# PEER block of a two-block layer: expert columns in pieces of 256, routing search in pairs of heads, one comparison for both one-hots

## The chip, the core and the metric

The kernel runs on one core of one Trainium2 chip. The metric is device time in microseconds (us); lower is better. Three runs of the kernel before took 3589.3 to 3594.07 us, median 3592.75 us. The engines are named as in the profile: PE is TensorE, PEld its weight loads, DVE VectorE, ACT ScalarE, POOL GpSimd, SP SyncE (which here only issues DMAs).

## The reference, cut to what matters

Two blocks run on 256 tokens of 2048 features in float32. The change touches the PEER part of the second block alone: a product-key search picks 16 of 16384 experts for each of 8 heads and each token, and the experts' outputs are added with softmax gates.

```python
PEER_HEADS = 8; PEER_NKEYS = 128; PEER_HALF = 128; PEER_TOPK = 16
q = (xn @ w_pq).reshape(B, S, PEER_HEADS, 2, PEER_HALF)
s1 = jnp.einsum('bshd,hnd->bshn', q[..., 0, :], sub_k1)
s2 = jnp.einsum('bshd,hnd->bshn', q[..., 1, :], sub_k2)
v1, i1 = lax.top_k(s1, PEER_TOPK)
v2, i2 = lax.top_k(s2, PEER_TOPK)
cand = (v1[..., :, None] + v2[..., None, :]).reshape(B, S, PEER_HEADS, PEER_TOPK * PEER_TOPK)
vs, ci = lax.top_k(cand, PEER_TOPK)
e1 = jnp.take_along_axis(i1, ci // PEER_TOPK, axis=-1)
e2 = jnp.take_along_axis(i2, ci % PEER_TOPK, axis=-1)
eidx = e1 * PEER_NKEYS + e2
gates = jax.nn.softmax(vs, axis=-1)
# per token: act = gelu(expert_u[eidx] . x);  out = sum(act * gates * expert_v[eidx])
```

## The kernel before, in words

**Weights.** All large products run on PE with each operand split into a high and a low part. Weights stream from HBM in pieces of 512 KB. For each piece `_load` issues a DMA on the SP queue into `raw`, `_emit` lets ACT copy `raw` to `hi` and DVE subtract to get `lo`, and PE then uses both. `raw`, `hi` and `lo` have three buffers each, and `get` keeps two pieces ahead of the one that PE uses. While `self.share` is true, POOL makes the `lo` part of every second piece instead of DVE (line 341 in the trace).

**All experts are computed.** The kernel doesn't gather experts. It multiplies the tokens with all 16384 columns of `expert_u` (the u products: 32 quads of 512 experts, 8 pieces `w_u` each), applies Gelu, multiplies with a dense gate matrix that is zero where an expert isn't chosen, and multiplies the result with `expert_v` (the v products: 16 groups of 1024 experts, 16 pieces `w_v` each). `mmH` does the u products: per weight tile one matmul of 512 moving columns (line 390, `hi`) and one of 256 (line 391, `lo`). `mmB` does the v products with three matmuls (lines 362 to 364). A piece of `w_u` has 8 tiles of 128 rows and 128 columns; a piece of `w_pq` has 4 of 256 columns. Both need 16 matmuls.

**The gates.** `scores` finds the top 16 of each head's two key halves, as soon as a block of `w_pq` columns is done. `route` waits for all of these, then adds the candidates, finds their top 16 and picks the indices for four heads at a time, and makes `routeT` (the two indices and the gate of each of the 128 choices, per token). `dense` turns that into the gate matrix in 64 groups of 4 tokens: `onehot` builds `Bt` (one comparison on DVE, 512 columns) and `At` (four instructions on DVE that compare and multiply with the gate, 128 columns each), PE multiplies them (line 1977; four calls in the program, eight records in the trace), ACT copies the result from PSUM into `G`, and after every fourth group ACT issues a DMA that writes `G` to DRAM (`gdram`). When all 16 of these are written, `gated` can load a quad's gates `Gq` (on the SP queue), multiply them into the activations `act` on DVE, and split the result into `wh` (ACT) and `wl` (DVE), which a v group needs for its two quads.

**What sets the order.** The programs of the engines are written out by one Python thread. After each weight piece `pump` adds 2.6 to two credits, one for DVE and one for ACT, each held between -2 and 2, takes off what the meters of the two engines say was issued since (a fixed part, 0.066 for DVE and 0.2 for ACT, and a part per element), and runs steps of the waiting background tasks (`scores`, `route`, `dense`, `gated`) while both credits are positive. `finish(task)` runs a task to its end at once, and with it whatever it waits for; nothing else stands between. `peer_order` says which u quads and v groups follow each other: before, v group 0 comes after quad 11, then one v group after every second quad. Before a v group, `finish` is called for its two quads' `gated`. Every engine then executes its own program strictly in this order, and waits where a semaphore isn't there yet.

**Lines.** Every DVE and ACT instruction passes through the meter and so has line 37; they are told apart by their tiles.

Of the kernel before, what the change touches and what calls it, by code (L numbers as in the profile page):

```python
# [6 lines left out]
F32 = mybir.dt.float32  # L7
# [130 lines left out]
def layout(inp):  # L138

    f = {k: np.asarray(v) for k, v in inp.items()}  # L140
    A = {}
# [55 lines left out]
    eu = f["expert_u_2"][0].reshape(128, 128, 2, 8, 128)  # L197
    A["w_u"] = eu.transpose(0, 2, 4, 3, 1).reshape(256, 128, 1024)
# [867 lines left out]
LAG = 10  # L1066


class Block1(Mixers):
# [14 lines left out]
    def order(self):  # L1084
# [40 lines left out]
        for kind, i in self.peer_order():  # L1125
            if kind == "u":
                p("w_u", 8 * i, 8, kk=8, w=128)
            else:
                p("w_v", 16 * i, 16)
# [694 lines left out]
NACT = 11  # L1824
# [3 lines left out]
class Block3(Block2):  # L1828
    def peer(self, X):
        nc, V, S, G, A, bg, tc = self.nc, self.V, self.S, self.G, self.A, self.bg, self.tc  # L1830
        h, st = self.h, self.st
# [11 lines left out]
        v12 = rp.tile([128, 2, 2, 8, 16], F32, name="v12")  # L1843
        i12 = rp.tile([128, 2, 2, 8, 16], U32, name="i12")
        qT = [None] * 4

# [14 lines left out]
        def scores(c):  # L1861

            for t in range(2):
# [10 lines left out]
                for j in (0, 2):  # L1874
                    top16([(s[:, j + z], 128, v12[:, t, z, 2 * c + j // 2], i12[:, t, z, 2 * c + j // 2]) for z in range(2)])
                    yield

        self.share = True
        tk = []

        def take(i, ps):
# [5 lines left out]
            if z:  # L1887
                tk.append(bg.add(scores(c)))
# [6 lines left out]
        def route():  # L1895
            yield lambda: all(t[3] for t in tk)
            for t in range(2):
                f12 = rp.tile([128, 2, 8, 16], F32, name="f12")
                V.tensor_copy(f12, i12[:, t])
                cd = rp.tile([128, 4, 16, 16], F32, name="cand")  # L1900
                eq = cd.rearrange("p a b c -> p (a b c)").rearrange("p (m k) -> p m k", k=16)
                vs = rp.tile([128, 8, 16], F32, name="vs")
                ci = rp.tile([128, 8, 16], U32, name="ci")
# [228 lines left out]
```

## Time and profile before

| | |
|---|---|
| median of three runs | 3592.75 us |
| profiled execution, its own time | 3589.29 us |
| its span in the trace | 3587.5 us |
| PE busy | 3508.7 us (98%) |
| DVE busy | 2450.7 us (68%) |
| ACT busy | 1702.7 us (47%) |
| POOL busy | 383.6 us (11%) |

Times in the trace count from the start of the span. The pieces of `w_pq` are loaded from 1836 us on, those of `w_u` from 1932 us; the first v group's pieces from 2313 us. Busy shares are shares of the span. A matmul's record is as long as the matmul is in the array, and records overlap, so what a matmul costs is read from start to start of two that follow each other. A granted clock (PEclk) of 1.00 is 2.4 GHz, 0.5 is 1.2 GHz; a stretch in between had some of both. An idle time in brackets names what ended it.

### The profile page before, as it was taken

What the parts mean: (1) busy time and instruction counts of PE and PEld (TensorE: products, weight loads), DVE (VectorE), ACT (ScalarE), POOL (GpSimd) and SP (SyncE); (2) the same over time, 40 slices, a digit from 0 to 9 for tenths busy, and PEclk for the clock granted to TensorE, in tenths of its full rate; (3) what the DMA queues carried; (4) which work ended last, traced back from release to release, by engine and by line L of the source; (5) the groups of instructions that cost most, each with busy time, mean ns of one, the idle gap of its engine ahead of it and who ended that gap; (6) DMA issues with size and microseconds to landing.
All of it is one profiled execution on the core that took longest, in us unless ns stands there. A gap on an engine that the chain in (4) does not pass through costs nothing.

```text
span 3587.5 us, 47390 instructions
## 1 busy us (share of the span) xinstructions
PE 3508.7 (98%) x18330; PEld 2981.0 (83%) x18330; DVE 2450.7 (68%) x3245; ACT 1702.7 (47%) x1974; POOL 383.6 (11%) x404
## 2 busy tenths in 40 slices
PE   8899999999999999999999889899999999999999
PEld 8788877888888888889788778788888888888887
DVE  7987575466775577667667999766655656556665
ACT  4345543445554455545454455544444444444454
POOL 6900000000000000021214333100000000000000
PEclk9999999999999999999999999999999999999999
DMA  6455554665566555565455446666666666667765
GB/s 224 135 157 164 171 174 131 194 205 188 188 200 196 188 186 188 192 194 178 130 173 175 144 162 214 203 201 202 202 200 200 205 201 203 201 201 214 217 192 183
DMA packets 244794, 670.05 MB, mean 187 GB/s; under 512 B 86180, under 2 KB 86628, under 8 KB 242392
## 3 DMA queue, kind: packets, MB, share of 16 engines
q1 hardware_dynamic: 239144, 639.59, 56.2%
q10 hardware_dynamic: 2736, 17.32, 1.2%
q0 software_dynamic: 2688, 10.12, 1.0%
q8 instruction: 143, 2.34, 0.3%
q14 instruction: 83, 0.68, 0.1%
HBM read 648.07 MB, written 18.87 MB: 186 GB/s over the span
## 4 chain that ended last, share of the span: by engine, by line
PE 87%; DVE 9%; issue 1%; ACT 1%; DMA 1%; POOL 0%; SPq 0%; DVEq 0%; ACTq 0%; POOLq 0%
PE mm L390 21%; PE mm L362 16%; PE mm L363 16%; PE mm L364 16%; PE mm L391 11%; DVE lo L37 3%; DVE At L37 1%; PE mm L377 1%; PE mm L376 1%; PE mm L378 1%; PE m L1977 1%; DVE Bt L37 1%; ACT hi L37 1%; DVE cand L37 1%; PE m L492 1%
## 5 line engine op out<-in xcount | busy, mean ns | idle before, releaser
L37 DVE TENSOR_TENSOR lo<-raw,hi 128x1024 fp32r<-128x1024 f32 (+3 forms) x1123 | 1379.9, 1231 | 929.1 <-ACT hi L37 926.1
L37 ACT ACTIVATE hi<-raw 128x1024 fp32r<-128x1024 f32 (+1 forms) x1185 | 1247.0, 1054 | 1463.4 <-PE mm L364 806.7
L390 PE MATMUL mm<-xt,hi 128*128 128x512 f32 x3712 | 1319.9, 400 | 9.5 <-ACT hi L37 9.5
L391 PE MATMUL mm<-xt,lo 128*128 128x256 f32 x3712 | 1043.7, 281 | 15.2 <-DVE lo L37 14.9
L390 PEld LDWEIGHTS mm<-xt,hi 128*128 128x128 f32 x3712 | 701.5, 189 | 176.7 <-ACT hi L37 9.8
L391 PEld LDWEIGHTS mm<-xt,lo 128*128 128x128 f32 x3712 | 704.7, 190 | 19.3 <-DVE lo L37 18.3
L363 PE MATMUL mm<-lo,wh 128*128 128x512 f32 x1024 | 398.7, 389 | 1.3 <-DVE lo L37 1.3
L362 PE MATMUL mm<-hi,wh 128*128 128x512 f32 x1024 | 399.0, 390 | 0.6 <-ACT hi L37 0.6
L364 PE MATMUL mm<-hi,wl 128*128 128x512 f32 x1024 | 398.6, 389 | 0.0
L363 PE MATMUL mm<-lo,x 128*128 128x512 f32 x576 | 227.0, 394 | 10.1 <-DVE lo L37 10.1
L362 PE MATMUL mm<-hi,x 128*128 128x512 f32 x576 | 230.1, 399 | 2.7 <-ACT hi L37 2.7
L363 PEld LDWEIGHTS mm<-lo,wh 128*128 128x128 f32 x1024 | 192.2, 188 | 41.7 <-DVE lo L37 2.0
L364 PE MATMUL mm<-hi,x 128*128 128x512 f32 x576 | 226.1, 393 | 0.0
L362 PEld LDWEIGHTS mm<-hi,wh 128*128 128x128 f32 x1024 | 192.2, 188 | 40.7 <-ACT hi L37 1.0
L364 PEld LDWEIGHTS mm<-hi,wl 128*128 128x128 f32 x1024 | 192.2, 188 | 40.3
L341 POOL TENSOR_TENSOR lo<-raw,hi 128x1024 fp32r<-128x1024 f32 x62 | 159.5, 2572 | 336.9 <-ACT hi L37 296.6
L362 PE MATMUL mm<-hi,xt 128*128 128x512 f32 x376 | 147.2, 392 | 0.1
L363 PE MATMUL mm<-lo,xt 128*128 128x512 f32 x376 | 146.5, 390 | 0.0
L364 PE MATMUL mm<-hi,xt 128*128 128x512 f32 x376 | 146.4, 389 | 0.0
L363 PEld LDWEIGHTS mm<-lo,x 128*128 128x128 f32 x576 | 109.3, 190 | 34.1 <-DVE lo L37 12.6
L362 PE MATMUL mm<-hi,acth 128*128 128x512 f32 x352 | 137.2, 390 | 0.0
L364 PE MATMUL mm<-hi,actl 128*128 128x512 f32 x352 | 137.0, 389 | 0.0
(561 smaller groups left out, 4355.5 us busy)
## 6 DMA issues: line engine op xcount, KB each, us to landing
raw<-in_w_u_dram SPq DMA_DIRECT2D x256, 512.0 KB, 4.0
raw<-in_w_v_dram SPq DMA_DIRECT2D x256, 512.0 KB, 4.2
raw<-in_w_up_dram SPq DMA_DIRECT2D x176, 512.0 KB, 3.8
raw<-in_w_g_dram SPq DMA_DIRECT2D x96, 512.0 KB, 3.4
raw<-in_w_dn_dram SPq DMA_DIRECT2D x88, 512.0 KB, 4.3
raw<-in_w_o_dram SPq DMA_DIRECT2D x64, 512.0 KB, 3.4
raw<-in_w_b_dram SPq DMA_DIRECT2D x32, 512.0 KB, 3.6
raw<-in_w_br_dram SPq DMA_DIRECT2D x32, 512.0 KB, 3.4
```

What stands on the lines that cost most here:

```text
L37: return f(*a, **k)
L341: sub.tensor_sub(lo[:, ks], raw[:, ks], hi[:, ks].bitcast(F32))
L362: nc.tensor.matmul(ps[:, t, :n], xh[:, sl], hi[:, i, :n], start=s, stop=False)
L363: nc.tensor.matmul(ps[:, t, :n], xh[:, sl], lo[:, i, :n], start=False, stop=False)
L364: nc.tensor.matmul(ps[:, t, :n], xl[:, sl], hi[:, i, :n], start=False, stop=e)
L376: nc.tensor.matmul(ps[:, c, :], hi[:, i, sl], xh, start=s and c % 2 == 0, stop=False, **kw)
L377: nc.tensor.matmul(ps[:, c, :], hi[:, i, sl], xl, start=False, stop=False, **kw)
L378: nc.tensor.matmul(ps[:, c, :], lo[:, i, sl], xh, start=False, stop=e, **kw)
L390: nc.tensor.matmul(ps[:, c], hi[:, i, sl], xx, start=s, stop=False, **kw)
L391: nc.tensor.matmul(ps[:, c, 256:], lo[:, i, sl], xx[:, :256], start=False, stop=e, **kw)
L492: self.nc.tensor.transpose(ps[:, c, t * 128:t * 128 + 128], src(t)[:, c * 128:c * 128 + 128], self.ident)
L1977: nc.tensor.matmul(ps[:, i], Bs[:, i], As[:, i], start=True, stop=True)
```

## The change

What it does, in the order of the diff:

- `w_u` is laid out in pieces of 4 tiles of 256 columns instead of 8 of 128, and the u products use `prodH` as `w_pq` does.
- v group 0 comes after quad 14 (`FIRST` = 15) instead of after quad 11, and v group 1 follows it at once. The activations of the first four quads then lie in the pool `a4`.
- DVE's meter counts 0.15 as the fixed part from the PEER block on (0.066 before).
- A new background task `pairs` does the candidates' search for two heads and 128 tokens as soon as their scores are searched; `route` keeps the softmax and the transposes. Score tasks go ahead of the others.
- `onehot` makes both one-hots in one comparison of 1024 columns on DVE (tile `AB`); the multiplication with the gate becomes four copies of 128 columns on ACT, with a scale per partition.
- `share` ends before the first `w_u` piece is used instead of after `dense`. In the programs as built, POOL makes 16 `lo` parts instead of 62, all among the `w_pq` pieces.

```diff
-    eu = f["expert_u_2"][0].reshape(128, 128, 2, 8, 128)
-    A["w_u"] = eu.transpose(0, 2, 4, 3, 1).reshape(256, 128, 1024)
+    eu = f["expert_u_2"][0].reshape(64, 2, 128, 4, 4, 128)
+    A["w_u"] = eu.transpose(0, 3, 5, 4, 1, 2).reshape(256, 128, 1024)
...
-LAG = 10
+NACT = 11
+FIRST = NACT + 4
...
-                p("w_u", 8 * i, 8, kk=8, w=128)
+                p("w_u", 8 * i, 8, kk=4, w=256)
...
-        out, v = [], 0
-        for q in range(32):
+
+        out = [("u", q) for q in range(FIRST)] + [("v", 0), ("v", 1)]
+        v = 2
+        for q in range(FIRST, 32):
             out.append(("u", q))
-            if q >= LAG and (q - LAG) % 2 == 1:
+            if (q - FIRST) % 2 == 1:
                 out.append(("v", v))
                 v += 1
-        out += [("v", g) for g in range(v, 16)]
-        return out
+        return out + [("v", g) for g in range(v, 16)]
...
-NACT = 11
...
+        V.fixed = 0.15
...
         qT = [None] * 4
+        e3 = rp.tile([128, 2, 3, 8, 16], F32, name="e3")
+        v12 = rp.tile([128, 2, 8, 2, 16], F32, name="v12")
+        i12 = rp.tile([128, 2, 8, 2, 16], U32, name="i12")
...
-                for j in (0, 2):
-                    top16([(s[:, j + z], 128, v12[:, t, z, 2 * c + j // 2], i12[:, t, z, 2 * c + j // 2]) for z in range(2)])
+                for j in range(2):
+                    h = 2 * c + j
+                    top16([(s[:, 2 * j + z], 128, v12[:, t, h, z], i12[:, t, h, z]) for z in range(2)])
                     yield
+                tk.append(bg.add(pairs(c, t)))
+
+        def pairs(c, t):
+
+            hs = slice(2 * c, 2 * c + 2)
+            f12 = rp.tile([128, 2, 2, 16], F32, name="f12", bufs=2)
+            cd = rp.tile([128, 2, 16, 16], F32, name="cand", bufs=2)
+            eq = cd.rearrange("p a b c -> p (a b c)").rearrange("p (m k) -> p m k", k=16)
+            V.tensor_copy(f12, i12[:, t, hs])
+            V.tensor_tensor(cd, v12[:, t, hs, 0, :, None].to_broadcast([128, 2, 16, 16]),
+                            v12[:, t, hs, 1, None, :].to_broadcast([128, 2, 16, 16]), op=OP.add)
+            yield
+            ci = rp.tile([128, 2, 16], U32, name="ci", bufs=2)
+            top16([(cd[:, j].rearrange("p a b -> p (a b)"), 256, e3[:, t, 2, 2 * c + j], ci[:, j]) for j in range(2)])
+            yield
+            V.tensor_scalar(ab[:, 0], ci, 4, None, op0=OP.logical_shift_right)
+            V.tensor_scalar(ab[:, 1], ci, 15, None, op0=OP.bitwise_and)
+            V.tensor_copy(abf, ab)
...
+            for z in range(2):
+                V.tensor_tensor(eq, io16[:, None, :].to_broadcast([128, 32, 16]),
+                                abf[:, z].rearrange("p h j -> p (h j)")[:, :, None].to_broadcast([128, 32, 16]),
+                                op=OP.is_equal)
+                V.tensor_mul(cd, cd, f12[:, :, z, None, :].to_broadcast([128, 2, 16, 16]))
+                yield
+                V.tensor_reduce(e3[:, t, z, hs].rearrange("p h j -> p (h j)"), eq, axis=AX.X, op=OP.add)
+                yield
...
-                tk.append(bg.add(scores(c)))
+                bg.add(scores(c))
+                bg.tasks.insert(sum(x in bg.tasks for x in sc), bg.tasks[-1])
+                sc.append(bg.tasks.pop())
...
-            yield lambda: all(t[3] for t in tk)
+            yield lambda: all(t[3] for t in sc + tk)
+            mx = rp.tile([128, 2, 8, 1], F32, name="gmx")
+            V.tensor_copy(mx, e3[:, :, 2, :, 0:1])
             for t in range(2):
...
-                for g in range(2):
-                    hs = slice(4 * g, 4 * g + 4)
-                    V.tensor_tensor(cd, v12[:, t, 0, hs, :, None].to_broadcast([128, 4, 16, 16]),
-                                    v12[:, t, 1, hs, None, :].to_broadcast([128, 4, 16, 16]), op=OP.add)
-                    yield
-                    for h0 in (0, 2):
-                        top16([(cd[:, hh].rearrange("p a b -> p (a b)"), 256, vs[:, 4 * g + hh], ci[:, 4 * g + hh])
-                               for hh in (h0, h0 + 1)])
...
-                e3 = rp.tile([128, 3, 128], F32, name="e3")
...
-                        V.tensor_tensor(eq, io16[:, None, :].to_broadcast([128, 64, 16]),
-                                        abf[:, z, hs].rearrange("p h j -> p (h j)")[:, :, None].to_broadcast([128, 64, 16]),
-                                        op=OP.is_equal)
-                        yield
-                        V.tensor_mul(cd, cd, f12[:, z, hs, None, :].to_broadcast([128, 4, 16, 16]))
-                        yield
-                        V.tensor_reduce(e3[:, z, ms], eq, axis=AX.X, op=OP.add)
-                        yield
-                g3 = e3[:, 2].rearrange("p (h j) -> p h j", h=8)
+                g3 = e3[:, t, 2]
-                V.tensor_sub(g3, vs, vs[:, :, 0:1].to_broadcast([128, 8, 16]))
+                V.tensor_sub(g3, g3, mx[:, t].to_broadcast([128, 8, 16]))
...
-                    nc.tensor.transpose(ps[:, z], e3[:, z], self.ident)
+                    nc.tensor.transpose(ps[:, z], e3[:, t, z].rearrange("p h j -> p (h j)"), self.ident)
...
-                Bs = gp.tile([128, 4, 128], F32, name="Bt", tag="Bt", bufs=2)
-                As = gp.tile([128, 4, 128], F32, name="At", tag="At", bufs=2)
-                ts = slice(4 * n, 4 * n + 4)
-                V.tensor_tensor(Bs, self.iota[:, None, :].to_broadcast([128, 4, 128]),
-                                r_[:, 1, ts, None].to_broadcast([128, 4, 128]), op=OP.is_equal)
+
+                AB = gp.tile([128, 2, 4, 128], F32, name="AB", tag="AB", bufs=2)
+                V.tensor_tensor(AB, self.iota[:, None, None, :].to_broadcast([128, 2, 4, 128]),
+                                r_[:, 0:2, 4 * n:4 * n + 4, None].to_broadcast([128, 2, 4, 128]), op=OP.is_equal)
                 for i in range(4):
-                    t = 4 * n + i
-                    V.tensor_scalar(As[:, i], self.iota, r_[:, 0, t:t + 1], r_[:, 2, t:t + 1],
-                                    op0=OP.is_equal, op1=OP.mult)
-                return Bs, As
+                    S.activation(AB[:, 0, i], AB[:, 0, i], AF.Copy, scale=r_[:, 2, 4 * n + i:4 * n + i + 1])
+                return AB
...
+                AB = nxt
                 for i in range(4):
-                    nc.tensor.matmul(ps[:, i], Bs[:, i], As[:, i], start=True, stop=True)
...
-            self.room["W"] += 1
-            self.share = False
...
+        self.share = False
         for kind, i in self.peer_order():
             if kind == "u":
                 for z in range(2):
-                    ps = self.mm_ps([128, 2, 512])
-                    for e in range(2):
-                        for s in range(2):
-                            hi, lo = self.get("w_u")
-                            self.mmH(ps[:, e:e + 1], hi, lo, 8 * s, X, s == 0, s == 1)
-                            bg.pump()
+                    ps = self.prodH("w_u", X, 16)
                     if z == 0:
-                        if i >= NACT:
+                        if i >= FIRST:
                             bg.finish(wt[i - NACT])
-                        a = pact.tile([128, 4, 256], F32, name="act")
+                        a = self.a4([128, 4, 256], name="act") if i < FIRST - NACT else pact.tile([128, 4, 256], F32, name="act")
...
-            self.room["W"] += 2
+            self.room["W"] += 3 if i == 1 else 2
```

What becomes of the order, at three places. Names: `m_...` is the PSUM tile of a gate group; `mm` that of a product; numbers are the program's buffer numbers.

PE, in the last quad ahead of v group 0. Before (the last four of the last seven gate groups, in the middle of quad 11, then the next u piece):

```order
L1977 MATMUL m_19631<-At,Bt 128x128 x4
L1977 MATMUL m_19644<-At,Bt 128x128 x4
L1977 MATMUL m_19657<-At,Bt 128x128 x4
L1977 MATMUL m_19671<-At,Bt 128x128 x4
L390 MATMUL mm<-xt,hi 128x512
L391 MATMUL mm<-xt,lo 128x256
```

After (behind the last piece of quad 14 come 38 such gate rows, of which the last three stand here, and then v group 0):

```order
L1978 MATMUL m_20318<-AB 128x128 x4
L1978 MATMUL m_20330<-AB 128x128 x4
L1978 MATMUL m_20343<-AB 128x128 x4
L362 MATMUL mm<-hi,wh 128x512
L363 MATMUL mm<-lo,wh 128x512
L364 MATMUL mm<-hi,wl 128x512
```

Before, 7 gate groups stand together there, and the other 57 lie between u pieces; after, 38 stand together (rows `m_19876` to `m_20343`), and 26 lie between u pieces.

DVE, at the same place. Before:

```order
L37 TENSOR_TENSOR Bt<-iota,routeT 128x512
L37 TENSOR_SCALAR At<-iota,routeT 128x128 x4
L37 TENSOR_TENSOR Bt<-iota,routeT 128x512
L37 TENSOR_SCALAR At<-iota,routeT 128x128 x4
L37 TENSOR_TENSOR act<-act,Gq 128x1024
L37 TENSOR_TENSOR wl<-act,wh 128x1024
L37 TENSOR_TENSOR act<-mm,act 128x512
L37 TENSOR_TENSOR act<-act,R 128x512
L37 TENSOR_TENSOR lo<-raw,hi 128x1024 x4
L37 TENSOR_TENSOR act<-mm,act 128x512
```

After:

```order
L37 TENSOR_TENSOR lo<-raw,hi 128x1024 x2
L37 TENSOR_TENSOR AB<-iota,routeT 128x1024
L37 TENSOR_TENSOR lo<-raw,hi 128x1024
L37 TENSOR_TENSOR AB<-iota,routeT 128x1024
L37 TENSOR_TENSOR act<-mm,act 128x512
L37 TENSOR_TENSOR act<-act,R 128x512
L37 TENSOR_TENSOR AB<-iota,routeT 128x1024 x36
L37 TENSOR_TENSOR act<-act,Gq 128x1024
L37 TENSOR_TENSOR wl<-act,wh 128x1024
L37 TENSOR_TENSOR act<-act,Gq 128x1024
```

The `lo` parts, which before stand among the one-hots until shortly ahead of the end, are gone from the last 36 one-hots, and the four `At` instructions of a group have gone to ACT.

ACT, at the same place. Before:

```order
L37 ACTIVATE G<-m_19644 128x4x128
L1979 DMA gdram<-G 128x2048
L37 ACTIVATE G<-m_19657 128x4x128
L37 ACTIVATE G<-m_19671 128x4x128
L1990 DMA gdram<-G 128x2048
L37 ACTIVATE wh<-act 128x1024
L37 ACTIVATE act<-mm 128x512
L37 ACTIVATE hi<-raw 128x1024 x4
L37 ACTIVATE act<-mm 128x512
L37 ACTIVATE wh<-act 128x1024
```

After:

```order
L37 ACTIVATE AB<-AB,routeT 128x128 x4
L37 ACTIVATE G<-m_19842 128x4x128
L37 ACTIVATE hi<-raw 128x1024
L1980 DMA gdram<-G 128x2048
L37 ACTIVATE AB<-AB,routeT 128x128 x4
L37 ACTIVATE act<-mm 128x512
L37 ACTIVATE act<-act 128x1024
L37 ACTIVATE G<-m_19876 128x4x128
L37 ACTIVATE AB<-AB,routeT 128x128 x4
L37 ACTIVATE G<-m_19893 128x4x128
```

Four scaled copies (`AB<-AB,routeT`) now stand between two copies of `G`, and the last `hi` of the u pieces and of the first two v pieces stands ahead of all the 38 groups' copies of `G`.

## Rows read from the trace of the kernel before

**Rows 1.** Stretch, length, busy us (count) of PE, PEld, DVE, ACT, POOL; PEclk, DMA, GB/s.

```profile
1950.00:2100.00 150.00, 130.22 (x705) 110.59 (x703) 142.12 (x275) 62.51 (x67) 56.36 (x22) 0.97 0.46 151
2100.00:2305.00 205.00, 195.59 (x1266) 175.75 (x1267) 197.50 (x370) 120.78 (x127) 61.21 (x24) 0.99 0.55 195
2320.00:2340.00 20.00, 17.58 (x69) 13.90 (x70) 12.73 (x13) 8.02 (x10) 0.00 (x0) 0.82 0.67 188
...
2340.00:3410.00 1070.00, 1069.68 (x5285) 903.27 (x5284) 651.90 (x583) 478.91 (x478) 0.56 (x1) 1.00 0.67 204
```

**Rows 2.** What PE waited for, 1950 to 2340 us: us, times, longest.

```profile
PE mm L391 <- DVE lo L37: 14.9, 9, 3.3
PE mm L390 <- ACT hi L37: 9.5, 1, 9.5
```

**Rows 3.** PE's instructions by group, 1950 to 2320 us: count, busy us, mean ns.

```profile
L390 PE MATMUL mm<-xt,hi 128*128 128x512 f32 x738 | 271.1, 408 | 0.0
L1977 PE MATMUL m<-At,Bt 128*128 128x128 f32 x512 | 69.7, 279 | 7.7 <-DVE At L37 7.4 <-ACT G L37 0.3
```

**Rows 4.** PE in order of time (start, length): `w_pq`; then a gate group and `w_u`.

```profile
1882.36 0.39 PE L390 MATMUL mm<-xt,hi 128*128 128x512 f32 x1
...
1884.44 0.39 PE L390 MATMUL mm<-xt,hi 128*128 128x512 f32 x1
...
2295.13 1.95 PE L1977 MATMUL m<-At,Bt 128*128 128x128 f32 x16
...
2305.54 0.39 PE L390 MATMUL mm<-xt,hi 128*128 128x512 f32 x1
...
2310.05 0.40 PE L390 MATMUL mm<-xt,hi 128*128 128x512 f32 x1
```

**Rows 5.** DVE's instructions by group, 1833 to 2310 us.

```profile
L37 DVE TENSOR_SCALAR At<-iota,routeT 128x128 f32<-128x128 f32 x256 | 96.8, 437 | 0.0
L37 DVE TENSOR_TENSOR lo<-raw,hi 128x1024 fp32r<-128x1024 f32 x67 | 87.3, 1303 | 37.8 <-ACT hi L37 37.7
L37 DVE TENSOR_TENSOR Bt<-iota,routeT 128x512 f32<-128x512 f32 x64 | 56.8, 887 | 0.3 <-PE m L1977 0.3
```

**Rows 6.** ACT in order of time: scaled copies of 256 columns; a `G` and what follows.

```profile
16.99 0.89 ACT L37 ACTIVATE x<-xraw,mixg 128x256 fp32r<-128x256 f32 x2
...
2291.10 1.06 ACT L37 ACTIVATE G<-m 128x512 f32<-128x512 f32 x1 [2.63 <-PE m L1977]
2291.94 1.08 ACT L37 ACTIVATE hi<-raw 128x1024 fp32r<-128x1024 f32 x1
```

**Rows 7.** ACT by group, 1950 to 2345 us: an instruction of 128 columns without scale.

```profile
L37 ACT ACTIVATE e<-e 128x128 f32<-128x128 f32 x2 | 0.6, 310 | 7.9 <-DVE e L37 7.9
```

**Rows 8.** DVE in order of time, among the last gate groups.

```profile
2301.13 0.68 DVE L37 TENSOR_TENSOR Bt<-iota,routeT 128x512 f32<-128x512 f32 x1
2301.73 1.10 DVE L37 TENSOR_SCALAR At<-iota,routeT 128x128 f32<-128x128 f32 x4
2302.76 0.68 DVE L37 TENSOR_TENSOR Bt<-iota,routeT 128x512 f32<-128x512 f32 x1
```

**Rows 9.** The way from the last gate group to the first `wh` (engine q: its queue).

```profile
2303.84 1.17 PE L1977 MATMUL m<-At,Bt 128*128 128x128 f32 x8 [0.46 <-DVE At L37]
...
2306.13 0.33 ACTq L1990 DMA_DIRECT2D gdram<-G  x1
...
2310.14 0.39 SPq L2007 DMA_DIRECT2D Gq<-gdram  x1
...
2314.85 1.23 DVE L37 TENSOR_TENSOR act<-act,Gq 128x1024 f32<-128x1024 f32 x1 [10.39 <-DMA Gq<-gdram]
...
2316.11 1.06 ACT L37 ACTIVATE wh<-act 128x1024 fp32r<-128x1024 f32 x1 [10.01 <-DVE act L37]
```

**Rows 10.** PE in order of time, after its longest wait.

```profile
2322.08 0.63 PE L390 MATMUL mm<-xt,hi 128*128 128x512 f32 x1
...
2322.72 0.63 PE L390 MATMUL mm<-xt,hi 128*128 128x512 f32 x1
```

More of the change, by code (lines that the diff above doesn't have):

```diff
@@ L1873, in scores @@
                 yield
-                for j in (0, 2):
-                    top16([(s[:, j + z], 128, v12[:, t, z, 2 * c + j // 2], i12[:, t, z, 2 * c + j // 2]) for z in range(2)])
+                for j in range(2):
+                    h = 2 * c + j
+                    top16([(s[:, 2 * j + z], 128, v12[:, t, h, z], i12[:, t, h, z]) for z in range(2)])
                     yield
+                tk.append(bg.add(pairs(c, t)))
[11 more added lines that the diff above has]
+            yield
+            ab = rp.tile([128, 2, 2, 16], U32, name="ab", bufs=2)
+            abf = rp.tile([128, 2, 2, 16], F32, name="abf", bufs=2)
+            V.tensor_scalar(ab[:, 0], ci, 4, None, op0=OP.logical_shift_right)
[9 more added lines that the diff above has]
+                V.tensor_reduce(e3[:, t, z, hs].rearrange("p h j -> p (h j)"), eq, axis=AX.X, op=OP.add)
+                yield
         self.share = True
-        tk = []
+        sc, tk = [], []
         def take(i, ps):
@@ L1895, in route @@
         def route():
-            yield lambda: all(t[3] for t in tk)
+            yield lambda: all(t[3] for t in sc + tk)
+            mx = rp.tile([128, 2, 8, 1], F32, name="gmx")
+            V.tensor_copy(mx, e3[:, :, 2, :, 0:1])
             for t in range(2):
[L1898 to L1903, printed above, removed]
-                for g in range(2):
-                    hs = slice(4 * g, 4 * g + 4)
-                    V.tensor_tensor(cd, v12[:, t, 0, hs, :, None].to_broadcast([128, 4, 16, 16]),
-                                    v12[:, t, 1, hs, None, :].to_broadcast([128, 4, 16, 16]), op=OP.add)
-                    yield
-                    for h0 in (0, 2):
-                        top16([(cd[:, hh].rearrange("p a b -> p (a b)"), 256, vs[:, 4 * g + hh], ci[:, 4 * g + hh])
-                               for hh in (h0, h0 + 1)])
-                        yield
-                ab = rp.tile([128, 2, 8, 16], U32, name="ab")
-                abf = rp.tile([128, 2, 8, 16], F32, name="abf")
-                V.tensor_scalar(ab[:, 0], ci, 4, None, op0=OP.logical_shift_right)
-                V.tensor_scalar(ab[:, 1], ci, 15, None, op0=OP.bitwise_and)
-                V.tensor_copy(abf, ab)
-                yield
-                e3 = rp.tile([128, 3, 128], F32, name="e3")
-                for z in range(2):
-                    for g in range(2):
-                        ms, hs = slice(64 * g, 64 * g + 64), slice(4 * g, 4 * g + 4)
-                        V.tensor_tensor(eq, io16[:, None, :].to_broadcast([128, 64, 16]),
-                                        abf[:, z, hs].rearrange("p h j -> p (h j)")[:, :, None].to_broadcast([128, 64, 16]),
-                                        op=OP.is_equal)
-                        yield
-                        V.tensor_mul(cd, cd, f12[:, z, hs, None, :].to_broadcast([128, 4, 16, 16]))
-                        yield
-                        V.tensor_reduce(e3[:, z, ms], eq, axis=AX.X, op=OP.add)
-                        yield
-                g3 = e3[:, 2].rearrange("p (h j) -> p h j", h=8)
@@ L1974, in dense @@
                 ps = self.m1([128, 4, 128])
-                Bs, As = nxt
+                AB = nxt
                 for i in range(4):
-                    nc.tensor.matmul(ps[:, i], Bs[:, i], As[:, i], start=True, stop=True)
+                    nc.tensor.matmul(ps[:, i], AB[:, 1, i], AB[:, 0, i], start=True, stop=True)
                 if full is not None and n % 4 == 2:
```

2 lines of the change are left out of this document (removed).

## The prediction, made before the changed kernel was run

> **What bounds the kernel now.** I read the busy times by stretch first. From 2340 us to 3410 us PE is busy 1069.68 of 1070 us [rows 1]: there the kernel is its matmuls, and nothing that DVE, ACT or a DMA does faster shortens it. The time to win lies in the routing and the gates. Between 1950 and 2305 us DVE is busy 339.6 of 355 us and PE 325.8; from 2320 to 2340 us PE works at a granted clock of 0.82 on average [rows 1]. PE's own waits come next: it waits for `lo` parts that DVE is late with (14.9 us in 9 waits) and once for 9.5 us for a `hi` [rows 2], which stands in ACT's queue behind the first `wh`.
>
> How much PE loses in all is counted from its work. A pair of u matmuls (lines 390 and 391) takes 0.347 us from start to start (13 pairs from 2305.54 to 2310.05), a record of a gate matmul 1.95 / 16, less the last one's overhang, 0.111 us [rows 4]. From 1950 to 2320 us there are 738 pairs and 512 gate records [rows 3]: with 0.35 for a pair, since the first one after a gate group takes a little longer, 738 x 0.35 + 512 x 0.111 = 258 + 57 = 315 us, and 14 further small matmuls make 317. The stretch is 370 us long, so 53 us are lost. From 2320 to 2340 us, 2.4 us are idle and 18% of 20 us, 3.6 us, go to the half clock [rows 1], where a pair takes 0.64 us (2322.08 to 2322.72) [rows 10]. **Lost before: 59 us.** PE's total work is the same after (the number of matmuls doesn't change), so the new time is the old one, less 59, plus what PE loses then.
>
> **The change part by part.**
>
> *Pieces of 256.* 16 matmuls per piece either way. `w_pq` has the new form already: 6 pairs from 1882.36 to 1884.44 are 0.347 us each, as those of `w_u` are [rows 4]. DMA bytes and the ACT and DVE instructions per piece are the same too. I count 0; 0.001 us a pair would be 2 us over 2048 pairs, either way.
>
> *POOL's `lo` parts and the one-hots.* DVE gives up `At` (96.8 us) and `Bt` (56.8 us) [rows 5], takes 64 comparisons of 1024 columns at about 1.2 us (the `lo` of 1024 columns is the nearest form, 1.30 us on average with POOL beside it, [rows 5]) and 46 more `lo` parts at the same: -154 + 77 + 55 = -22 us. The search is only cut differently (two heads instead of four), and part of it moves into the `w_pq` pieces, where PE loses nothing that the rows show. With a larger fixed part in the meter, the order puts less DVE work after each piece. So the losses to a late `lo` between 1950 and 2300 us should nearly go; I leave 2 us (0 to 5), and 2 us for 26 changes between u and gate matmuls.
>
> *A new chain in the interleaved groups.* In a piece that carries a gate group ACT does `hi` (1.06), DVE `lo` (1.2) and the comparison (1.2), and ACT the four scaled copies, which stand ahead of the next `hi`: with 1.3 us for these, 4.8 us against 2.8 + 0.9 = 3.7 us of PE. In the order 26 groups fall on 37 pieces: 26 x 4.8 + 11 x 1.06 = 136 us against 37 x 2.8 + 26 x 0.9 = 127 us. Two pieces of lead (5.6 us) take up part of the 9. I take 4 us, between 0 and 12.
>
> *The burst.* This decides. After, the order has 38 of the 64 gate groups in one row between the last u piece of quad 14 and v group 0; before, 7. They are drawn there because `finish` asks for quad 0's `wh`, which needs all 16 blocks of `gdram`, and the credits allow only 26 groups by then, since a group now costs ACT 4 x 0.31 + 0.63 = 1.87 by its meter, and each piece's 2.6 has to pay 1.06 for a `hi` first. Between these groups PE has nothing else. Who sets their pace? On ACT four scaled copies and one `G`. The nearest scaled copy from SBUF to SBUF has 256 columns: two in 0.89 us, of which one lasts 0.49, so 0.40 from start to start [rows 6]. From 128 columns (0.31 us, [rows 7]) to the 1024 of `hi` (about 1.06) a column costs 0.00084 us, so 128 fewer take off 0.11: 0.29 us each. `G` lets the next instruction start 0.84 us after it [rows 6]. 4 x 0.29 + 0.84 + a quarter of a DMA issue of 0.33 [rows 9] = 2.08, say 2.1 us. DVE needs 1.2 us for a group and PE 8 x 0.111 = 0.89, both of which fit in. So 38 x 2.1 = 80 us, of which PE works 34: **46 us lost.** From below: copies as cheap as the unscaled one of 0.31 us with 0.1 overlap, 1.77 us a group, 33 us lost; from above: none overlaps, 2.7 us, 69 us. I take 46, nearest to the scaled row. At the head of the burst ACT first waits for the last u piece, adds, and does a Gelu: 2 us.
>
> Where the multiplication stands is also a rule of the Trainium skill (ScalarE: Activation LUTs, section Rules for kernel authors): multiplications belong on VectorE, not ScalarE. The rows of the burst before bear it out here: with compare and multiply in one DVE instruction a group takes 2302.76 - 2301.13 = 1.63 us [rows 8]. With that pace the 38 groups would lose 38 x (1.63 - 0.89) = 28 us and the sum below would be 18 us less; the order moves the multiplication to ACT, so 2.1 stands.
>
> *From the last group to the v products.* The way is the same as before, only nothing covers it: last gate matmuls from 2303.84 (0.9 us long), last `gdram` DMA at 2306.13 on ACT's queue, `Gq` from 2310.14 on SP's queue, DVE's multiplication at 2314.85, ACT's `wh` at 2316.11 to 2317.17 [rows 9]: 12.5 us. Before, two u pieces (5.6 us) ran in that time. Add 0.8 for `wl`, 3.5 for the half clock after such a pause (about 7 us of it were worked through before, at 0.64 instead of 0.35 a pair [rows 10]), and 1 for the third v piece, whose load now queues behind two `Gq` on SP. 18 us, between 14 and 24. On SP the first `Gq` moves behind 26 more weight loads; these are paced by `raw`'s three buffers and not by the queue, so that costs nothing, and POOL's queue has nothing left to delay. `Gq` of quads 2 and 3 come behind later loads with two pieces of lead: 0.
>
> **The sum.** Lost after: 2 + 2 + 4 + 46 + 2 + 18 = 74 us, against 59: +15 us. On the profiled execution's own 3589.3 us that gives 3604; the median of the runs lies 3.5 us above it, so I say 3607. What was won in the routing (about 40 us) is paid back in the burst.
>
> **Rivals.** (1) *The burst is cheap, faster than before.* If ACT's copies and `G` overlap so well that a group takes 1.4 us, the burst loses 19 us, the sum is 47 and the time 3577 to 3581. It turns to faster by over 0.2% at 38 x (p - 0.89) + 28 < 52, that is at p below 1.52 us. Against it: `G` alone takes 0.84 [rows 6], which leaves 0.15 for each copy beside the DMA issue, and no row of ACT has that. (2) *It evens out.* Copies at the unscaled price (1.77 us a group) and a way to the v products of 16 us: 2 + 2 + 4 + 33 + 2 + 16 = 59, which is no change, 3589 to 3593; with 1.95 us a group it is 7 us more. For it: both ends are in the rows. (3) *The chain also binds.* ACT to DVE and back with 4.8 us a piece in the interleaved part, where the lead is used up early, and ACT's waits for other engines break the overlap in the burst (2.3 us): 2 + 2 + 12 + 54 + 3 + 24 = 97, +38 us, 3627 to 3631. For it: every group needs two changes of engine more than before. (4) *The change doesn't do what it says*: gates ready at quad 15. By the order they aren't; that is the forecast itself.
>
> **How the numbers follow.** 0.2% of the time, about 7 us, is what a measurement of this kernel can tell from no change. Forecast (3600 to 3617) 0.53, chain and slow burst (up to 3636) 0.24, even (3586 to 3600) 0.16, faster 0.07. So slower 0.77, same 0.16, faster 0.07. The range leaves out the fast rival and part of the even case below and the end of the slow one above: 3592 to 3632.
>
> **What would show it.** In the trace after: line 391's waits for DVE's `lo` gone between 1950 and 2300 us (right: under 5 us); 304 records of the gate matmuls without a u matmul among them, 75 to 90 us long, ACT busy throughout and PE under half; groups 2.0 to 2.2 us apart; then a pause of 12 to 14 us that ends with `wh`. POOL with 16 `lo` parts. Wrong would be: groups under 1.6 us apart; PE waits for `hi` or `lo` of over 15 us among the first 26 groups; or PE waiting after 2450 us, where I expect none beyond the 0.3 us of before.

## The result and the profile after

The kernel after takes 3621.13 us (median of 4 runs, 3619.2 to 3624.63) against 3591.11 us: a ratio of 1.0084, 95% interval 1.0066 to 1.0101. It is slower, inside the range, by 30 us where 15 were forecast. The profiled execution took 3624.63 us, its span 3622.8 us, 35.3 more than the span before. The busy time by stretch (us of PE, PEld, DVE, ACT, POOL, then granted clock, DMA share, GB/s), to be read beside [rows 1]:

```profile
1950.00:2180.00 230.00, 227.49 (x1300) 197.72 (x1299) 195.17 (x400) 107.95 (x116) 0.00 (x0) 1.00 0.57 183
2180.00:2337.00 157.00, 143.31 (x841) 124.11 (x840) 89.91 (x85) 103.70 (x186) 0.00 (x0) 0.98 0.47 158
2345.00:2416.00 71.00, 49.16 (x282) 42.49 (x282) 43.75 (x36) 71.00 (x180) 0.00 (x0) 0.96 0.32 131
2416.00:2440.00 24.00, 11.54 (x40) 8.82 (x40) 7.58 (x7) 7.51 (x9) 0.00 (x0) 0.64 0.77 221
2440.00:3440.00 1000.00, 998.51 (x4883) 840.76 (x4882) 611.07 (x543) 443.76 (x441) 0.56 (x1) 1.00 0.66 205
```

In the routing PE now works nearly throughout. Among the interleaved gate groups (2180 to 2337 us) its records leave 14 us free (its starts, below, show 22 lost) though neither DVE nor ACT is full. In the row of groups ACT is busy for 71.00 of 71 us. Behind it come the pause and the half clock, and from 2440 us on PE is idle for 1.5 of 1000 us, next to nothing, as before. PE's waits between 1830 and 2500 us (total us, times, longest) and what ACT waits for, to be read beside [rows 2]:

```profile
ACT AB L37 <- DVE AB L37: 54.5, 27, 2.9
PE m L1978 <- ACT AB L37: 36.6, 46, 4.2
PE mm L362 <- ACT wh L37: 12.4, 1, 12.4
PE mm L391 <- DVE lo L37: 6.2, 9, 1.1
```

The wait for `lo` has shrunk from 14.9 to 6.2 us; in its place PE waits for ACT's scaled copies, and ACT for the comparison: 27 times, about once for each of the 26 groups that lie among u pieces.

One measure serves all kernels below: **PE's loss** in a stretch is the sum, over neighbouring matmuls, of the time from start to start less the usual time of the same two lines (0.233 + 0.117 us for a pair, 0.112 for a gate record). Usual is the lowest of the kernels' medians, so that a wait which one kernel always has at some place doesn't count as usual. "Routing" is 1830 us to the first gate matmul, "among" the gate groups between u pieces, "row" those without u matmuls between, with the wait at its head, "way" the 60 us after the last gate matmul. The kernel before has such a wait in its routing, at the small matmuls of the softmax (1950 to 2340 us):

```profile
PE m L1943 <- DVE e L37: 7.1, 2, 4.2
```

The expectations below leave it out: they reckon with 25.6 us for the routing before, and with 57 for the sum.

| kernel | routing | among | row (groups) | way | sum | median us |
|---|---|---|---|---|---|---|
| before | 32.0 | 12.7 | 3.4 (7) | 15.8 | 63.9 | 3591.1 |
| after | 7.9 | 22.2 | 47.2 (38) | 15.9 | 93.2 | 3621.1 |
| e1_behind | 8.4 | 3.1 | 43.6 (40) | 14.7 | 69.7 | 3597.9 |
| e3_oldhot | 5.4 | 1.3 | 32.9 (42) | 15.2 | 54.8 | 3583.3 |
| e7_newhot | 30.2 | 17.7 | 35.7 (33) | 15.3 | 98.9 | 3628.4 |
| e6_lag10 | 7.6 | 3.3 | 61.2 (57) | 15.1 | 87.2 | 3615.9 |
| e4_route | 45.6 | 13.9 | none | 16.5 | 76.1 | 3596.2 |
| e13_fixed | 11.4 | 8.4 | 23.2 (34) | 15.3 | 58.2 | 3587.2 |
| e5_share | 23.5 | 30.0 | 30.4 (24) | 14.3 | 98.2 | 3626.7 |
| e15_nopool | 5.3 | 1.8 | 27.6 (40) | 17.7 | 52.3 | 3576.1 |
| e8_pieces | 31.5 | 15.2 | 3.5 (7) | 15.6 | 65.8 | 3588.8 |
| e14_rate | 6.1 | 5.6 | none | 12.9 | 24.7 | 3550.8 |
| e17_high | 5.8 | 11.4 | none | 11.0 | 28.2 | 3555.4 |
| e18_oldsearch | 2.0 | 5.6 | none | 10.0 | 17.6 | 3543.7 |

The sums follow the spans of the profiled executions within some 6 us: after less before is 29.3 by the sums and 35.3 by the spans. Of the 6 us between them 3 lie ahead of all that was changed, since the first `w_pq` matmul starts at 1850.9 instead of 1847.8 us.

### The profile page after: what moved, and what is told of

It is laid out like the page before. It is cut to its first block, busy times and chain, and to the rows that moved or that the text cites. A ratio compares the mean times of both kernels' runs of the same rounds, so it can differ in the third digit from the quotient of the medians.

```text
span 3622.8 us, 47446 instructions
## 1 busy us (share of the span) xinstructions
PE 3523.5 (97%) x18330; PEld 2988.6 (82%) x18330; DVE 2407.5 (66%) x3088; ACT 1769.2 (49%) x2228; POOL 261.9 (7%) x358
## 4 chain that ended last, share of the span: by engine, by line
PE 88%; DVE 5%; ACT 4%; issue 2%; DMA 2%; POOL 0%; SPq 0%; ACTq 0%; DVEq 0%
PE mm L390 22%; PE mm L362 15%; PE mm L363 15%; PE mm L364 15%; PE mm L391 11%; ACT AB L37 2%; DVE lo L37 2%; PE mm L377 1%; PE mm L376 1%; PE mm L378 1%; ACT G L37 1%; ACT hi L37 1%; DVE AB L37 1%; PE m L858 1%; PE m L492 1%
## 5 line engine op out<-in xcount | busy, mean ns | idle before, releaser
L37 DVE TENSOR_TENSOR lo<-raw,hi 128x1024 fp32r<-128x1024 f32 (+1 forms) x1169 | 1431.3, 1227 | 963.1 <-ACT hi L37 959.9
L362 PE MATMUL mm<-hi,wh 128*128 128x512 f32 x1024 | 400.3, 391 | 12.4 <-ACT wh L37 12.4
L363 PE MATMUL mm<-lo,x 128*128 128x512 f32 x576 | 227.1, 394 | 14.1 <-DVE lo L37 13.9
L363 PE MATMUL mm<-lo,acth 128*128 128x512 f32 x352 | 137.0, 389 | 0.0
```

What stands on the lines that cost most here:

```text
L37: return f(*a, **k)
L362: nc.tensor.matmul(ps[:, t, :n], xh[:, sl], hi[:, i, :n], start=s, stop=False)
L363: nc.tensor.matmul(ps[:, t, :n], xh[:, sl], lo[:, i, :n], start=False, stop=False)
```

## The experiments

### Among the groups: a chain over two engines

The timeline of one group among u pieces in the kernel after (start, us, engine; in brackets the idle time before and its releaser):

```profile
2300.15 1.28 ACT L37 ACTIVATE AB<-AB,routeT 128x128 f32<-128x128 f32 x4 [2.49 <-DVE AB L37]
2300.61 1.36 PE L1978 MATMUL m<-AB 128*128 128x128 f32 x8 [0.24 <-ACT AB L37]
2301.34 1.04 ACT L37 ACTIVATE hi<-raw 128x1024 fp32r<-128x1024 f32 x1
2302.41 1.23 DVE L37 TENSOR_TENSOR lo<-raw,hi 128x1024 fp32r<-128x1024 f32 x1 [2.35 <-ACT hi L37]
2303.55 1.22 DVE L37 TENSOR_TENSOR AB<-iota,routeT 128x1024 f32<-128x1024 f32 x1
2304.86 1.28 ACT L37 ACTIVATE AB<-AB,routeT 128x128 f32<-128x128 f32 x4 [1.51 <-DVE AB L37]
2305.32 1.36 PE L1978 MATMUL m<-AB 128*128 128x128 f32 x8 [0.53 <-ACT AB L37]
```

The next copies start 4.71 us after these: copies, `hi`, `lo`, comparison, copies, with DVE idle for 2.35 us in between and ACT for 1.51. The chain was in the prediction (4.8 us); what it costs PE was not. If this reading is right, the copies need only go behind the next `hi`:

```diff
+                    yield 1
+                    scaled(n + 1, nxt)
```

(`scaled` holds the four copies that stood at the end of `onehot`.)

> The kernel after, with one thing moved: the four scaled copies of a gate group are issued on ACT one piece later than the comparison, so behind the next hi and no longer ahead of it. By the order 24 groups then lie between u pieces and 40 in one row (27 and 37 in the kernel after). Theory A (the 24.7 us lost among the interleaved groups are the chain: copies wait for the comparison, the comparison stands behind lo, lo waits for hi, hi stands behind the copies): the chain is cut, at most 5 us stay, and three more groups in the row cost 3 us: 3621 - 20 + 3 = about 3604 us, and ACT's waits for the comparison among the interleaved groups fall from 2 us each to nearly none. Theory B (they are lost because DVE now makes every lo part alone and is late with lo and comparison): nothing is gained, 3621 to 3625 us. On both the row of groups keeps its 1.96 us a group.

3597.88 us, 1.0023 times before (1.0014 to 1.0033); 22.2 us among the groups became 3.1, and ACT's waits for the comparison fell as foretold:

```profile
ACT AB L37 <- DVE AB L37: 6.9, 10, 2.9
```

Theory B falls: DVE had as many `lo` parts to make as before this edit. Then the one-hots of the kernel before in the kernel after (the diff's block `onehot` taken back):

> The kernel after with the one-hots of the kernel before: DVE makes one comparison for Bt and four compare-and-multiply instructions for At, ACT makes nothing of them. By the order 22 groups lie between u pieces and 42 in one row. Theory A (ACT's part in the one-hots is what costs, by its place in the chain and by the pace of 1.96 us): chain 24.7 -> 4 us, the 42 groups at the 1.63 us of the row before lose 42 x 0.74 = 31 us instead of 37, head of the row 9.5 -> 3: about 3621 - 33 = 3588 us. Theory B (DVE is the late engine among the interleaved groups, since POOL gives it no help): the old one-hots take DVE longer, so the interleaved groups lose 25 us or more, and the total is 3609 us or more.

3583.30 us, 0.998 (0.997 to 0.999), 38 us under the kernel after. A group in the row costs 0.78 us instead of 1.24 (each with its share of the head). And the other way round, the new one-hots alone in the kernel before:

> The kernel before with the new one-hots alone (one comparison of both on DVE, four scaled copies on ACT); search, meter, POOL, pieces and order as before. By the order 31 groups lie between u pieces and 33 in one row. Theory A (a group with its copies on ACT costs PE 0.8 us among u pieces by the chain and 1.1 in a row by ACT's pace): routing 25.6 as before, among 31 x 0.8 = 25 instead of 13, row 33 x 1.1 + 8 = 44 instead of 3, way 16: 111 against 57, about 3644 us. Theory D (DVE is the engine that runs late, and what it is relieved of helps): no more lost among u pieces than the 13 us of before, 3620 us or less.

3628.42 us, 1.0111 (1.0094 to 1.0128): 38 us slower. Theory D falls; theory A was too high by 16 us: 7 among the u pieces, where a group cost 0.57 us and not 0.8, and 8 in the row, 35.7 us and not 44. **The new one-hots alone cost about as much as they cost in the kernel after.**

### The order of u and v

`peer_order` and the first `W` room taken back to those of before:

> The kernel after with the order of u and v groups of the kernel before (first v group after quad 11). By the order 7 groups lie between u pieces and 57 in one row, and one more quad of u pieces follows the row ahead of the first v group. Theory A (a group costs PE about 1 us wherever it lies, 0.9 among u pieces by the chain and 1.0 in the row by ACT's pace, and only the way to the v products depends on the order): row 57 x 1.01 = 58, interleaved 7 x 0.9 = 6, routing 5, head 9, way 4 with the u quad as cover, sum 82 against 93 of the kernel after: about 3610 us. Theory C (the long row of groups comes from putting v later, and costs only there): the row gets longer by 20 groups but starts earlier, and the total is near the kernel before, 3591 us or less; or, if the row alone counts, 3621 + 20 = 3641 us.

3615.91 us, 1.0071 (1.0053 to 1.0089): 5 us under the kernel after. The row of 57 costs 1.07 us a group, so a group costs about the same wherever it lies, and theory C falls. Missed was the way: 15.1 us, not 4, though four u pieces lie behind the row. PE waits 9.6 us for their `hi`, which stands behind the first `wh` in ACT's queue, as in the kernel before [rows 2].

### The routing: which part brought the 24 us?

First the new search alone in the kernel before (`scores`, `pairs`, `take`, `route` of the diff):

> The kernel before with the new search alone: pairs of heads, the sums and indices of two heads begun as soon as their scores are there; one-hots, POOL, pieces and order stay as before. Theory A: of the 30 us that PE loses between 1830 and 2100 us in the kernel before, 5 stay, as in the kernel after: 3591 - 25 = 3566 us. Theory B (the search only gains in the kernel after because the meter's larger fixed part puts less DVE work after a piece): the DVE work moves into the w_pq pieces, lo parts are late there instead, and the gain is under 8 us: 3583 to 3591 us.

3596.21 us, 1.0018 (1.0009 to 1.0028): both theories fall, the kernel is 6 us slower. In its trace the routing loses 13.6 us more, 5.4 of them in PE's waits for `qT`, which the kernel before doesn't have; but that execution took 3604.61 us, 8 above the median. Then the meter's line alone:

```diff
+        V.fixed = 0.15
```

> The kernel before with one line of the change: the meter's fixed part for a DVE instruction raised from 0.066 to 0.15 us in this stage. Search, one-hots, POOL's lo parts, pieces and order stay. By the order the routing's DVE work is spread over more pieces, 30 gate groups lie between u pieces and 34 in one row (7 before). Theory M (the larger fixed part alone is what makes room for the lo parts in the routing): PE's loss from 1830 us to the first gate matmul falls from 25.6 us to 8, as in the kernel after; the row loses 34 x 0.78 = 27 us instead of 3, among the u pieces 8 instead of 13, the way to the v products 16 as before: 59 lost against 57, about 3592 us. Theory P (POOL's lo parts are what is late in the routing): the 25.6 us stay, and the row comes on top: about 3610 us.

3587.17 us, 0.9987 (0.9978 to 0.9997): the routing falls to 11.4 us, near what theory M has, and the row pays it back. But the kernel after with POOL's `lo` parts given back (`self.share = False` moved to the end of the gates) speaks against M as the whole of it:

> The kernel after with POOL making every second lo part until the gates are done, as in the kernel before. By the order 40 groups lie between u pieces and 24 in one row. Theory M (the meter made the room in the routing): the loss in the routing stays at 8 us; 40 groups among u pieces lose 0.82 us each by the chain, 33 us; the row 24 x 1.1 + 9 = 35; way to the v products 16: 92 us, about 3620 us. Theory P (POOL's lo parts come late): the routing loses 25 us again, and groups whose lo POOL makes lose more than 0.82 us each: 3637 us or more.

3626.65 us, 1.0107 (1.009 to 1.0124), between the two theories: with the same meter and search the routing loses 23.5 instead of 7.9 us. The trace shows longer instructions. The same DVE groups from 1955 to 2110 us (busy us, mean ns, then DVE's idle time before them), first of the kernel after, without POOL:

```profile
L37 DVE TENSOR_TENSOR act<-act,R 128x512 f32<-128x512 f32 x13 | 9.0, 692 | 0.4
L37 DVE TENSOR_TENSOR act<-mm,act 128x512 f32<-128x512 f32 x13 | 8.9, 687 | 3.7 <-ACT act L37 3.6
L37 DVE TENSOR_TENSOR cand<-io,abf 128x512 f32<-128x512 f32 x9 | 6.2, 688 | 0.1
L37 DVE CAST f<-i 128x64 f32<-128x64 uint32 x5 | 0.9, 189 | 0.0
```

then of e5_share, with POOL:

```profile
L37 DVE TENSOR_TENSOR act<-act,R 128x512 f32<-128x512 f32 x13 | 16.9, 1296 | 0.4
L37 DVE TENSOR_TENSOR act<-mm,act 128x512 f32<-128x512 f32 x13 | 8.9, 681 | 3.2 <-ACT act L37 3.2
L37 DVE TENSOR_TENSOR cand<-io,abf 128x512 f32<-128x512 f32 x13 | 14.2, 1091 | 0.2
L37 DVE CAST f<-i 128x64 f32<-128x64 uint32 x6 | 8.3, 1384 | 0.0
```

Instructions with two inputs, both from SBUF, last up to twice as long on average, a small cast seven times. The one that reads `mm` from PSUM does not change, nor does the sum over `cand`, with one input (679 and 680 ns). So one more run, POOL's `lo` parts taken from the kernel before from the first u piece on, and nothing else:

```diff
         ssp = self.ssp5 = self.small([128, 2, 4], "ssp")
+        self.share = False
```

> The kernel before with POOL making no lo parts from the first u piece on; search, meter, one-hots, pieces and order stay. By the order 40 gate groups then lie in one row. Theory Q (POOL's lo parts give DVE nothing: where POOL works, DVE's two-input instructions from SBUF last longer, lo 1.42 instead of 1.22 us, act x R 1.14 instead of 0.69, so what DVE must make itself it gets back in shorter instructions): the loss in the routing stays near the 25.6 us of before, within 6 us, the row of 40 loses 40 x 0.78 + 2 = 33, among the u pieces 5, way 15: 79 against 57, 3608 to 3616 us. Theory R (DVE loses the help and is later): routing 40 us or more, 3625 us or more. Theory P (POOL was what delayed the routing): routing 10 us or less, 3597 us or less.

3576.05 us, 0.9961 (0.9945 to 0.9976), with the old search and the old meter: the routing loses 5.3 us, and the kernel is 14 us faster though 40 groups now lie in a row. Theory P, on which I had not bet, is right in its numbers: **without POOL's help `lo` is hardly late.** From 1955 to 2110 us (columns as in the first view above), in the kernel before and then in e15_nopool:

```profile
1955.00:2110.00 155.00, 133.56 (x716) 113.50 (x715) 147.25 (x261) 61.98 (x67) 57.84 (x22) 0.96 0.46 150
```

```profile
1955.00:2110.00 155.00, 153.27 (x872) 132.77 (x871) 146.72 (x280) 74.36 (x80) 0.00 (x0) 1.00 0.56 184
```

DVE is busy equally long, 147 us, but PE gets through 872 matmuls instead of 716. In the kernel before, eight groups of DVE instructions last longer there than in e15_nopool, 31 us in sum. Two of them in the kernel before and then in e15_nopool:

```profile
L37 DVE TENSOR_TENSOR lo<-raw,hi 128x1024 fp32r<-128x1024 f32 x22 | 31.1, 1415 | 6.8 <-ACT hi L37 6.8
L37 DVE TENSOR_TENSOR act<-act,R 128x512 f32<-128x512 f32 x11 | 12.6, 1144 | 0.4
```

```profile
L37 DVE TENSOR_TENSOR lo<-raw,hi 128x1024 fp32r<-128x1024 f32 x54 | 64.9, 1218 | 5.4 <-ACT hi L37 4.2 <-PE m L1943 1.0
L37 DVE TENSOR_TENSOR act<-act,R 128x512 f32<-128x512 f32 x14 | 9.7, 693 | 0.5
```

The 31 us are more than the 22 x 1.22 = 27 us which POOL's 22 `lo` parts spare DVE: this much of theory Q holds. The meter counts what POOL spares and not what it costs, so the program puts more on DVE than fits.

The order changes as well: without POOL the meter charges every `lo` to DVE, and the routing spreads over 63 u pieces ahead of the first gate group instead of 46 (e13_fixed: 59, with POOL at work). How much of the gain is the spreading and how much the shorter instructions, no run parts.

### Pieces of 256

The layout of `w_u` and `prodH` alone, in the kernel before:

> The kernel before with the w_u pieces of 256 columns by 4 blocks of rows alone. Same matmuls, same bytes, same splits. My term for it was 0, at most 2 us either way: 3588 to 3592 us, ratio 0.9995 to 1.0005. The rival is a price that the prediction did not see (another pitch of the pairs, or DMAs that land later): 3593 us or more, with the L390 to L391 pitch no longer at 0.347 us a pair.

3588.80 us, ratio 1.0000 (0.9991 to 1.0009). The term 0 holds.

### What is left, and a faster kernel

e3_oldhot still has 42 groups in a row, because 2.6 us of credits a piece pay for too few. With more credits while the gates run:

```diff
             rp_.close()
+            bg.rate = 4.8
...
             gst["ready"] = True
+            bg.rate = RATE
```

(`pump` takes its credits from `self.rate`, which is `RATE` elsewhere.)

> The kernel after with the one-hots of the kernel before, and with credits of 4.8 us instead of 2.6 for every piece from the first gate group to the last one. By the order all 64 groups then lie between u pieces, one or two to a piece, and none in a row. DVE has 1.22 + 1.64 x 1.63 = 3.9 us a piece, PE 2.8 + 1.64 x 0.89 = 4.3. Theory A (what is left of the loss in e3_oldhot is the row, 32.9 us, and the way to the v products, 15): routing 6, among the u pieces 5 to 12, no row, way 15: about 30 us lost against 54 in e3_oldhot: 3556 to 3563 us. Theory D (DVE has no room for the groups among the pieces, and the row is only the same loss in another place): 35 us among the u pieces, 3583 us as e3_oldhot.

3550.77 us, 0.989 (0.9874 to 0.9907): the row is gone and the u pieces take the groups at 5.6 us; theory A was 5 us too careful. With the search of the kernel before on top:

> e14_rate with the search of the kernel before (four heads at a time, after all scores). Meter, POOL, one-hots and credits as in e14_rate; by the order the groups lie the same way. Theory M (the meter alone made the room in the routing, the search has no part in it): routing loses 6 to 10 us as in e14_rate, total within 4 us of it, 3547 to 3555 us. Theory S (without POOL the search two heads at a time is what keeps lo in time): routing loses 18 us or more, 3562 us or more.

**3543.74 us, 0.9871 (0.9856 to 0.9886), 46 us under before and the fastest here.** Theory S falls, and M too, by 3 us: the search does have a part, and the old one is 7 us better than the new, in the direction of e4_route. Why two heads at a time cost 4 us in the routing here stays open. Last, still more credits, so that u pieces cover the way:

> e14_rate with the credits that may be kept over raised from 2 to 3 us and those of a piece from 4.8 to 5.4 us while the gates run: by the order two groups to every u piece, and six u pieces behind the last group ahead of the first v group instead of one. DVE has 1.22 + 2 x 1.63 = 4.48 us a piece, PE 2.8 + 2 x 0.89 = 4.58. Theory W (the way to the v products, 12.9 us in e14_rate, is hidden by u pieces if its steps are drawn one at a time between them): 12 us less, about 3539 us. Theory X (the wh stands ahead of a hi in ACT's queue wherever it comes, as in the kernel before and in e6_lag10, both with u pieces behind the last group and 15 us lost): no gain, 3548 to 3553 us, with one wait of PE for hi or wh of over 8 us.

3555.43 us, 0.9908 (0.9893 to 0.9924). Theory W falls. X comes within 3 us, and its long wait is there, but not by its reason: the wait of 8.2 us for `wh` comes from a `hi` ahead of it on ACT, which waits for a v piece whose load stands behind the `Gq` loads on SP's queue:

```profile
2341.84 7.18 SPq L2015 DMA_DIRECT2D Gq<-gdram  x3
2355.20 1.06 ACT L38 ACTIVATE hi<-raw 128x1024 fp32r<-128x1024 f32 x1 [6.82 <-DMA raw<-in_w_v_dram]
2361.11 0.79 PE L366 MATMUL mm<-hi,wh 128*128 128x512 f32 x1 [8.17 <-ACT wh L38]
```

## Why the prediction was right, and where it was not

- **Direction and cause: right; the number is luck in part.** What the routing won was paid back by gate groups that wait for ACT. The loss before, 59 us from 1950 to 2340 us, measures 63.2 there. The sum after, 74, measures 93.2: too low were the chain by 18 us, the head of the row by 7.5 and the routing by 4, too high the burst by 8 and the way by 2. The time of 3621 us lies inside the range but above the forecast's own band (3600 to 3617), in that of rival 3 (up to 3636). That rival's sum of 97 is near by errors that cancel: its row (54) and way (24) are too dear, its chain (12) too cheap.
- **The burst: right, a little too dear.** Forecast were 2.1 us a group; the row runs at 1.96, ACT without a gap:

```profile
2413.53 1.07 ACT L37 ACTIVATE AB<-AB,routeT 128x128 f32<-128x128 f32 x3
2414.40 1.11 ACT L37 ACTIVATE G<-m 128x512 f32<-128x512 f32 x1
2415.22 1.34 ACT L37 ACTIVATE AB<-AB,routeT 128x128 f32<-128x128 f32 x4
2416.36 1.97 ACT L37 ACTIVATE G<-m 128x512 f32<-128x512 f32 x2
```

  From `G` to `G` 2416.36 - 2414.40 = 1.96 us: 0.82 for `G`, 1.14 for four copies. The row without its head loses 37.7 us, for 46. By the rule cited from the Trainium skill (ScalarE: Activation LUTs, section Rules for kernel authors) the multiplication belonged on DVE. With it there (e3_oldhot) a group takes 2351.05 - 2349.42 = 1.63 us from `Bt` to `Bt`, as in [rows 8], so the trace bears the rule out.
- **The head: 2 us forecast, 9.5 measured.** The step saw a u piece, an addition and a Gelu; one more pass through `hi`, `lo`, comparison and copies lies there as well, from 2338.05 to 2341.59 us, at whose end PE has waited 4.2 us.
- **The chain among the groups: 4 us forecast, 12 at most, 22.2 measured.** This is the step that failed, by its size: a piece without a group was put at ACT's `hi` alone, 1.06 us, and `G` and `act` were left out of the chain. ACT is busy for 103.70 of the 157 us from 2180 to 2337 us, and waits for the comparison for 52.0 us more, in 26 of the 27 waits shown above. So the chain runs without a break, and ACT's `hi` never waits there for PE to free a buffer. From copies to copies, 16 times with one piece between, take 5.0 us on average (4.71 in the lines above), 8 times with two pieces 7.1 and twice with three 8.9: each further piece costs some 2 us. One with two pieces:

```profile
2329.51 1.28 ACT L37 ACTIVATE AB<-AB,routeT 128x128 f32<-128x128 f32 x4 [1.88 <-DVE AB L37]
2330.70 1.04 ACT L37 ACTIVATE hi<-raw 128x1024 fp32r<-128x1024 f32 x1
2331.65 1.07 ACT L37 ACTIVATE G<-m 128x512 f32<-128x512 f32 x1
2332.51 1.06 ACT L37 ACTIVATE hi<-raw 128x1024 fp32r<-128x1024 f32 x1
2336.06 0.40 ACT L37 ACTIVATE AB<-AB,routeT 128x128 f32<-128x128 f32 x1 [2.49 <-DVE AB L37]
```

  With one piece `G` runs while DVE makes `lo` and the comparison; here the second `hi` waits behind it, so `G` adds its 0.86 us to that `hi`'s 1.0. In all 26 times with 38 pieces take 155 us, against 38 x 2.8 + 26 x 0.9 = 130 us of PE's work. The lead takes up the first of the difference, as the prediction had it: PE has lost 4 us by 2236 us and 18 more by 2336. Rival 3 had the mechanism and half the price.
- **Way to the v products: 18 forecast, 15.9 measured.** It is 15.8 in the kernel before too, where the prediction saw two u pieces (5.6 us) cover part of it. The last group's DMA, `Gq`, the product and `wh`, to be read beside [rows 9]:

```profile
2418.36 0.33 ACTq L1991 DMA_DIRECT2D gdram<-G  x1
2422.27 1.62 SPq L2006 DMA_DIRECT2D Gq<-gdram  x2
2427.15 1.23 DVE L37 TENSOR_TENSOR act<-act,Gq 128x1024 f32<-128x1024 f32 x1 [12.71 <-DMA Gq<-gdram]
2428.41 1.06 ACT L37 ACTIVATE wh<-act 128x1024 fp32r<-128x1024 f32 x1 [10.08 <-DVE act L37]
2429.52 0.80 PE L362 MATMUL mm<-hi,wh 128*128 128x512 f32 x1 [12.42 <-ACT wh L37]
```

- **The routing: near, for half the reason.** 4 us were left for it, 7.9 measured. The prediction credited the shorter one-hots and the meter. e13_fixed shows that the meter helps while POOL works, e15_nopool that taking POOL off is enough by itself, e4_route and e18_oldsearch that the new search costs. POOL's 46 `lo` parts were counted as 55 us more of DVE work, and what DVE gains when POOL is silent, 31 us in 155 us of the kernel before, was left out.
- **The signs.** 304 gate records without a u matmul among them last 80 us (2336.5 to 2416.8), for 75 to 90; the pause ends with `wh` after 12.4, for 12 to 14; POOL makes 16 `lo` parts; line 391 waits 4.6 us for `lo` between 1950 and 2300 us, for under 5. Missed: the groups are 1.96 us apart, for 2.0 to 2.2; PE's records fill 69% of the row, not under half; and PE waits 1.5 us in all after 2450 us, where 0.3 were expected. The sign set for rival 3, waits for `hi` or `lo` among the first groups, did not come, since PE waits there for the copies: the sign was named for the wrong tile.

## What to carry to other kernels

When a chain over two engines runs without a break, price every piece in it, those without a group too, with all that stands in the queue between and isn't hidden; and look whether one instruction can go behind the next one in its queue, which here gave back 19 us. Before an idle engine is given a share of DVE's work, or loses it, compare the durations of DVE's instructions with and without it: the rows of before had `lo` at 1.30 to 1.42 us beside POOL and 1.22 alone. A meter that spreads work by counted costs has to count that too. Taking one part of a change at a time showed a gain (POOL off, more credits), a zero (the pieces) and losses (one-hots on ACT, the new search, 5 us for the order) where the whole only showed 30 us.

## What the runs showed of the hardware

A DVE instruction can be held by a POOL instruction to the latter's end. In e4_route two small shifts, 0.35 us where POOL is silent (174 ns each on average in the kernel after), last 2.46 us beside a `lo` of POOL that ends 0.12 us before them:

```profile
1901.91 2.38 POOL L341 TENSOR_TENSOR lo<-raw,hi 128x1024 fp32r<-128x1024 f32 x1 [5.77 <-ACT hi L37]
1901.95 2.46 DVE L37 TENSOR_SCALAR ab<-ci 128x32 uint32<-128x32 uint32 x2
```

The Trainium skill (SBUF — State Buffer, section Who interferes with whom) states it: a DVE instruction with two SBUF inputs, or in a mode that uses both ports, contends with a GpSimd instruction that reads SBUF, and the second to come blocks until the first ends. The rows agree: 692 against 1296 ns with both inputs in SBUF, 687 against 681 ns with one in PSUM. In which mode the shifts ran, no run shows. The prediction did not weigh this rule.
